# A hybrid attention and SSD layer on one core: an eighth Strassen pair, two filler blocks fewer, a store and a pause moved

## The chip, the cores and the metric

The kernel runs on one core of a Trainium2 chip. The metric is the device time of one execution in microseconds. A measurement of this kernel can tell a difference of some 0.2% from none, which is 3.9 us.

## What is computed

One layer of a streaming encoder, for 1024 prompt tokens and 8 x 16 sample tokens, in 32-bit numbers (1152 tokens stand side by side, `NT`):

```python
h = rms_norm(x, norm_g) * (1 + scale) + shift
q, k, v, z_att, z_ssd, xbc, dt_raw, gates = split(h @ w_in)
att_branch = (attend(rms_norm(q), rms_norm(k), v) * silu(z_att)) @ w_att_proj
xs, bm, cm = split(silu(causal_dwconv(xbc)))
y, h_new = ssd_scan(xs, softplus(dt_raw + dt_bias), a, bm, cm, h0)
y = group_rms_norm((y + d_skip * xs) * silu(z_ssd))
merged = sigmoid(g_att) * att_branch + sigmoid(g_ssd) * (y @ w_ssd_proj)
out = x + gate * (merged @ w_out)
```

The inner width is 2048 for the SSD branch: 32 heads of 64, which the kernel takes in 16 pairs `p` of heads, four pairs to each of four groups that share B and C. The final states of the prompt (`out_hp`) and of the samples (`out_hs`) are outputs too.

## The kernel before

Weights come in blocks of 128 output columns. A **dense block** (`dense`, L474 on) multiplies such a block with all tokens: 8 pieces of the inner dimension, 3 groups of 384 tokens, and 3 products each, since every operand is split into a high and a low part in the fast 32-bit format (L489, L490, L492). That is 72 matmuls of 384 columns a block. The weights' high part is made by ScalarE (L374), the low part by VectorE (L375).

The program has these stages:

- The start: modulation, norm, the first block, four more dense blocks.
- **Strassen pairs** (`pairs`): two dense blocks are made together by Strassen's seven products instead of eight, each of 4 x 2 x 3 matmuls of 288 columns: 168 matmuls a pair (L880, L882, L883). `w_form` makes the sums of the weights on VectorE, the sums of the products are taken by VectorE (L844), activations by ScalarE (L855). `NPR` is the number of pairs, 7. After them one block is left that is made as a plain dense block (L999 and L1000 evict it if it is a z block, L1005 if it is a gate). Results are stored to DRAM and read back where they are needed.
- Attention, 8 units.
- The **SSD stage**, 16 pairs of heads. For each pair PE makes a dense block of x, VectorE runs its causal convolution (three L1531, then L1537 and L1538), and `main` of `ssd(p)` does the scan: transposes (L1754) scaled by VectorE (L1758), products to states (L1799), a chain of 14 small VectorE steps (L1808) that carries the state from chunk to chunk, products to outputs (L1830, L1837, L1855), VectorE steps on them (L1848, L1861, L1862), and the samples' new states (L1881), whose four products each need an operand that GpSimd masks (`masked`, L1788). Only two masked operands are held at a time: the third is made when the first has been used. Each group begins with two dense blocks for B and C with convolutions of their own, and products of them (L1669, L1675). It ends with a norm over the group, whose sums go through DRAM and whose inverse root GpSimd computes (L1156, then lines L328 to L334).
- Six dense blocks of gates, then the projections of attention (`att_dense`), of the SSD branch and of the output. `att_prep` loads the attention results (L1940) and splits them (L1927 on ScalarE, L1929 on VectorE).

**What sets the order.** Everything is written out in one order by a planner in the kernel (`run`). It draws dense matmuls from one generator, keeps a clock that counts the PE time it has written, and slips in steps of the SSD pairs, which wait on that clock (`pause`, `until`) as an allowance for the time that VectorE, ScalarE and GpSimd need. A `pause(4500)` between the second and the third of the samples' four products is such an allowance. The tool that builds the program may move instructions too, by its own schedule. Since a pair of heads needs more time on VectorE than on PE, the planner puts some further dense blocks into the SSD stage as **fillers**: `SLOTS` names the pairs after whose block of x a filler follows. `BLOCKS` is one list of the gate and z blocks: the first `4 + NEARLY` of them are made at the start, the next ones are the fillers, and the gates that are left follow the SSD stage.

Stores from GpSimd (`store`) and loads and stores from SyncE (`dma`) are issued in order, each on its queue, so an instruction that waits there holds up those behind it.

Of the kernel before, what the change touches and what calls it, by code (L numbers as in the profile page):

```python
# [12 lines left out]
P = 128  # L13
# [15 lines left out]
RW = HALO + NP + NB * (HALO + NS)  # L29
EPS = 1e-6  # L30
AHEAD = 2
NEARLY = 15
SLOTS = (('p', 1), ('p', 3), ('p', 6), ('p', 9), ('p', 11), ('p', 13), ('p', 15))
BLOCKS = [("gate", i) for i in range(4)] + [("z", p) for p in range(NPAIR)] + [("gate", i) for i in range(4, 16)]
AHEAD_BLOCKS = BLOCKS[:4 + NEARLY]
FILL = dict(zip(SLOTS, BLOCKS[4 + NEARLY:]))
NGATE = 4 + NEARLY + len(SLOTS) - NPAIR
NZ = 5
NPR = 7
TH = NT // 2  # L40
MH = TH // 2
BIG = -1e30
# [89 lines left out]
def trunk_kernel(ctx: ExitStack, tc: tile.TileContext, h):  # L132
# [182 lines left out]
    store = nc.gpsimd.dma_start  # L315
# [142 lines left out]
    for i in range(NZ):  # L458
        job(h["wall"][i])
    for i in range(NPR):  # L460
        job(*(h["wall"][NZ + 2 * i + j] for j in range(2)))
    for i in range(NZ + 2 * NPR, nz):
        job(h["wall"][i])
# [620 lines left out]
    def pause(t):  # L1084
        yield from until(clock[0] + t)

    def stored(*bufs):

        def wait():
            yield from pause(9000)  # L1090
            for b in bufs:
                b.free()
        urgent.append(wait())
# [520 lines left out]

    ngate = [max(4, 4 + NEARLY - NPAIR)]

# [68 lines left out]
    def ssd(p):  # L1685
# [51 lines left out]
        def main():  # L1737
# [6 lines left out]
            hst = yield from walloc(lay, "T", NP)  # L1744
# [69 lines left out]
            eb = alloc(lay, "T", NT)  # L1814
            for e in range(2):
                dma(eb.ap[e * HD:(e + 1) * HD], eacs_d[hds[e]:hds[e] + 1].to_broadcast([HD, NT]))
            store(h["out_hp"][p], hst.ap[:, 7 * P:])
            yield from pause(1200)
            yield from until(tm)

# [24 lines left out]
            for j in range(3):  # L1845
# [16 lines left out]
                nc.vector.tensor_tensor(x.ap[:, c2], x.ap[:, c2], eb.ap[:, c2], ALU.add)  # L1862
                yield 213 * n
            eb.free()
            stored(hst)
            yield from until(tz)

# [10 lines left out]
            for q in range(4):  # L1878
                j, i = q // 2, q % 2
                for w, b_ in enumerate(res["st"][j]):  # L1880
                    nc.tensor.matmul(pss_[j][:, 2 * i * P:2 * (i + 1) * P], b_.r, xm[q].r, start=w == 0, stop=w == 1)  # L1881
                xm[q].free()
                if q < 2:
                    xm.append(masked(q + 2))
                yield 215
                if q == 1:
                    yield from pause(4500)
                if i:
                    c = slice(4 * j * P, (4 * j + 4) * P)
                    nc.vector.tensor_tensor(h0.ap[:, c], h0.ap[:, c], pss_[j], ALU.add)  # L1890
# [323 lines left out]
```

## Time and profile before

| | |
|---|---|
| median of 3 runs | 1944.68 us (1944.65 to 1945.52) |
| profiled execution | 1943.42 us |
| its span | 1941.6 us |
| PE busy in the span | 1922.7 us (99%) |
| VectorE (DVE) busy | 1251.5 us (64%) |
| ScalarE (ACT) busy | 798.3 us (41%) |
| GpSimd (POOL) busy | 339.7 us (17%) |
| chain that ended last | PE 92%, DVE 3%, DMA 2%, ACT 1% |

The span is what the profile covers of the profiled execution, whose time is 1.8 us longer. PE stands for TensorE's matmuls. Busy shares are means over stages that differ, so a stage is read from the view of its own stretch. Ends of matmuls are modelled; the spacing of their starts is what a matmul costs.

### The profile page before, as it was taken

The numbers are of one execution on the slowest core, as the hardware profiler recorded it, in microseconds if no ns is written. First come the engines' busy times: TensorE is split into PE (matmuls) and PEld (weight loads), VectorE is DVE, ScalarE is ACT, GpSimd is POOL, SyncE is SP. The second block draws the span as 40 slices with busy tenths as digits, with TensorE's granted clock in tenths as the row PEclk, the third lists the DMA queues.
The fourth block names the chain that finished last, engine by engine and source line by source line (L and its number), as shares of the span: only waits on it lengthen the run. The fifth ranks groups of instructions, "written<-read, shape, count | busy, mean of one in ns | idle before, by whom it ended". The sixth has DMA issues, their size and how long they took to land.

```text
span 1941.6 us, 35765 instructions
## 1 busy us (share of the span) xinstructions
PE 1922.7 (99%) x14259; PEld 1842.4 (95%) x14259; DVE 1251.5 (64%) x2577; ACT 798.3 (41%) x1639; POOL 339.7 (17%) x615
## 2 busy tenths in 40 slices
PE   7999999999999999999999999999999999999999
PEld 5999999999899998998999999999999999999999
DVE  6756634555556456558597988888885434777732
ACT  7533324444454444545655546465453311111200
POOL 0000003213123131221022343242241300000000
PEclk9999999999999999999999999999999999999999
DMA  8222342343333333423345354554558742331341
GB/s 316 92 81 95 109 173 69 96 129 116 97 117 101 122 116 94 130 82 115 119 132 181 132 162 152 168 173 140 160 192 289 292 144 93 105 105 56 89 143 52
DMA packets 85966, 258.73 MB, mean 133 GB/s; under 512 B 14732, under 2 KB 15768, under 8 KB 85800
## 3 DMA queue, kind: packets, MB, share of 16 engines
q1 hardware_dynamic: 77416, 229.57, 36.5%
q0 software_dynamic: 8384, 26.88, 3.6%
q8 instruction: 112, 1.84, 0.4%
q14 instruction: 54, 0.44, 0.1%
HBM read 202.72 MB, written 53.68 MB: 132 GB/s over the span
## 4 chain that ended last, share of the span: by engine, by line
PE 92%; DVE 3%; DMA 2%; ACT 1%; issue 1%; POOL 0%; SPq 0%; ACTq 0%; DVEq 0%; POOLq 0%
PE d L489 11%; PE d L492 11%; PE d L490 11%; PE d L557 5%; PE d L555 5%; PE d L556 5%; PE s L489 4%; PE s L490 4%; PE s L492 4%; PE g L1311 3%; PE g L1334 3%; PE s L1390 2%; PE g L880 2%; PE g L883 2%; PE g L882 2%; PE g L490 1%
## 5 line engine op out<-in xcount | busy, mean ns | idle before, releaser
L489 PE MATMUL d<-rarena 128*128 128x384 f32 x1288 | 437.7, 340 | 0.0
L492 PE MATMUL d<-rarena 128*128 128x384 f32 x1288 | 434.2, 337 | 0.0
L490 PE MATMUL d<-rarena 128*128 128x384 f32 x1288 | 433.3, 336 | 0.0
L489 PEld LDWEIGHTS d<-rarena 128*128 128x128 f32 x1288 | 242.0, 188 | 4.1 <-issue 2.7
L492 PEld LDWEIGHTS d<-rarena 128*128 128x128 f32 x1288 | 241.9, 188 | 2.2 <-issue 2.0
L490 PEld LDWEIGHTS d<-rarena 128*128 128x128 f32 x1288 | 242.1, 188 | 0.8 <-issue 0.4
L557 PE MATMUL d<-va_att,rarena 128*128 128x384 f32 (+1 forms) x567 | 197.6, 349 | 0.0
L555 PE MATMUL d<-va_att,rarena 128*128 128x384 f32 (+1 forms) x567 | 196.7, 347 | 0.0
L556 PE MATMUL d<-va_att,rarena 128*128 128x384 f32 (+1 forms) x567 | 193.7, 342 | 0.0
L374 ACT ACTIVATE rarena<-arena 128x1024 fp32r<-128x1024 f32 x76 | 80.5, 1059 | 262.9 <-PE s L490 173.9
L489 PE MATMUL s<-rarena 128*128 128x384 f32 x488 | 165.6, 339 | 0.0
L490 PE MATMUL s<-rarena 128*128 128x384 f32 x488 | 164.2, 336 | 0.0
L492 PE MATMUL s<-rarena 128*128 128x384 f32 x488 | 163.3, 335 | 0.0
L1299 ACT ACTIVATE ma_att<-ma_att 128x640 f32<-128x640 f32 (+2 forms) x144 | 101.5, 706 | 135.8 <-DVE ma_att L1408 99.7
L1228 POOL TENSOR_SCALAR ma_att<-ma_att 128x16 f32<-128x16 f32 (+1 forms) x24 | 5.2, 218 | 707.3 <-DVE ma_att L1205 417.2
L557 PEld LDWEIGHTS d<-va_att,rarena 128*128 128x128 f32 x567 | 107.0, 189 | 3.9 <-issue 2.7
L555 PEld LDWEIGHTS d<-va_att,rarena 128*128 128x128 f32 x567 | 106.8, 188 | 2.7 <-issue 1.2
L375 DVE TENSOR_TENSOR rarena<-arena,rarena 128x1024 fp32r<-128x1024 f32 x76 | 93.3, 1227 | 22.6 <-ACT rarena L374 22.6
L556 PEld LDWEIGHTS d<-va_att,rarena 128*128 128x128 f32 x567 | 106.8, 188 | 0.5
L1531 DVE SCALAR_TENSOR_TENSOR ma_att<-ma_att,arena 128x1176 f32<-128x1176 f32 x63 | 93.9, 1491 | 9.4 <-ACT ma_att L1528 8.1
L489 PEld LDWEIGHTS s<-rarena 128*128 128x128 f32 x488 | 91.7, 188 | 1.3 <-issue 1.2
L490 PEld LDWEIGHTS s<-rarena 128*128 128x128 f32 x488 | 91.7, 188 | 0.8 <-issue 0.8
(437 smaller groups left out, 4128.0 us busy)
## 6 DMA issues: line engine op xcount, KB each, us to landing
arena<-in_wall_dram SPq DMA_DIRECT2D x85, 512.0 KB, 3.6
ma_att<-in_kc_dram SPq DMA_DIRECT2D x64, 256.0 KB, 4.3
ma_att<-in_vc_dram SPq DMA_DIRECT2D x64, 256.0 KB, 3.5
ma_att<-acs_d SPq DMA_DIRECT2D x23, 576.0 KB, 6.8
ma_att<-y_d SPq DMA_DIRECT2D x15, 576.0 KB, 6.3
arena<-in_wssd_dram SPq DMA_DIRECT2D x16, 512.0 KB, 4.5
z_d<-va_start SPq DMA_DIRECT2D x13, 576.0 KB, 2.8
ma_att<-eacs_d SPq DMA_DIRECT2D x26, 288.0 KB, 3.9
```

The source lines that it names most:

```text
L374: keep(nc.scalar.activation(hi.r[:, c], b.ap, AF.Copy))
L375: keep(nc.vector.tensor_tensor(lo.r[:, c], b.ap, hi.ap[:, c], ALU.subtract))
L489: nc.tensor.matmul(ps, hi.r[:, wc], kh.r[:, tok], start=k == 0, stop=False)
L490: nc.tensor.matmul(ps, hi.r[:, wc], kl.r[:, tok], start=False, stop=False)
L492: nc.tensor.matmul(ps, lo.r[:, wc], kh.r[:, tok], start=False, stop=k == nk - 1)
L555: nc.tensor.matmul(ps, kh.r[:, tok], wh, start=j == 0, stop=False)
L556: nc.tensor.matmul(ps, kh.r[:, tok], wl, start=False, stop=False)
L557: nc.tensor.matmul(ps, kl.r[:, tok], wh, start=False, stop=j == KT - 1)
L1299: nc.scalar.activation(p, p, AF.Exp, bias=sm_[:, 4 + e:5 + e], scale=-1.0, accum_out=sm_[:, 6 + e:7 + e])
L1311: nc.tensor.transpose(ps[:, s * P:(s + 1) * P], p[:, (j + s) * P:(j + s + 1) * P], ident)
L1334: late(nc.tensor.matmul(po[e * HD:e * HD + HD, a * P:(a + 1) * P], v.ap[:, vc:vc + HD], x.ap[:, o + i * P:o + (i + 1) * P], start=i == 0, ...
L1531: nc.vector.scalar_tensor_tensor(yc, r.ap[:, j:j + n], w4[:, i, j:j + 1], yc, ALU.mult, ALU.add)
```

## The change

- `NEARLY` goes from 15 to 17 and `NPR` from 7 to 8: two more blocks are made at the start, and all but one of the blocks after the first five are made in pairs. The blocks made at the start are now gates 0 to 3, all z blocks, and gate 4; the plain block after the pairs is gate 4, where it was z block 14.
- `SLOTS` has five entries where it had seven. The fillers are now gates 5 to 9, where they were z block 15 and gates 4 to 9. `NGATE` stays 10, so six gate blocks still follow the SSD stage.
- The store of the prompt's final state of a pair of heads is written some steps later, behind the VectorE steps on the outputs.
- The pause between the two halves of the samples' products is 6500 in place of 4500 on the planner's clock.

```diff
--- before.py
+++ after.py
@@ -29,14 +29,14 @@
 RW = HALO + NP + NB * (HALO + NS)
 EPS = 1e-6
 AHEAD = 2
-NEARLY = 15
-SLOTS = (('p', 1), ('p', 3), ('p', 6), ('p', 9), ('p', 11), ('p', 13), ('p', 15))
+NEARLY = 17
+SLOTS = (('p', 1), ('p', 3), ('p', 6), ('p', 10), ('p', 15))
 BLOCKS = [("gate", i) for i in range(4)] + [("z", p) for p in range(NPAIR)] + [("gate", i) for i in range(4, 16)]
 AHEAD_BLOCKS = BLOCKS[:4 + NEARLY]
 FILL = dict(zip(SLOTS, BLOCKS[4 + NEARLY:]))
 NGATE = 4 + NEARLY + len(SLOTS) - NPAIR
 NZ = 5
-NPR = 7
+NPR = 8
 TH = NT // 2
 MH = TH // 2
 BIG = -1e30
@@ -1814,7 +1814,6 @@
             eb = alloc(lay, "T", NT)
             for e in range(2):
                 dma(eb.ap[e * HD:(e + 1) * HD], eacs_d[hds[e]:hds[e] + 1].to_broadcast([HD, NT]))
-            store(h["out_hp"][p], hst.ap[:, 7 * P:])
             yield from pause(1200)
             yield from until(tm)
 
@@ -1862,6 +1861,7 @@
                 nc.vector.tensor_tensor(x.ap[:, c2], x.ap[:, c2], eb.ap[:, c2], ALU.add)
                 yield 213 * n
             eb.free()
+            store(h["out_hp"][p], hst.ap[:, 7 * P:])
             stored(hst)
             yield from until(tz)
 
@@ -1884,7 +1884,7 @@
                     xm.append(masked(q + 2))
                 yield 215
                 if q == 1:
-                    yield from pause(4500)
+                    yield from pause(6500)
                 if i:
                     c = slice(4 * j * P, (4 * j + 4) * P)
                     nc.vector.tensor_tensor(h0.ap[:, c], h0.ap[:, c], pss_[j], ALU.add)
```

Since the planner writes the order, the change moves instructions in the whole SSD stage. Up to the end of the seventh pair the order of PE is the same. Two places follow.

GpSimd's queue at the end of the third group, where the group's norm (L1156, L328 to L334) and the masks of pair 12 (L1788, the four operands of its products) meet; L1817 is the store of the prompt's state, L1639 that of a gate. Before:

```order
L1156 TENSOR_SCALAR ma_att<-ma_att 128x9
L328 MEMSET ma_att 128x9
L329 TENSOR_TENSOR ma_att<-ma_att 128x9
L331 TENSOR_TENSOR ma_att<-ma_att 128x9
L332 TENSOR_TENSOR ma_att<-ma_att 128x9
L333 TENSOR_SCALAR ma_att<-ma_att 128x9
L334 TENSOR_TENSOR ma_att<-ma_att 128x9
L1817 DMA out_hp_dram<-va_ssd 128x128
L331 TENSOR_TENSOR ma_att<-ma_att 128x9
L1788 TENSOR_TENSOR rarena<-rarena,arena 128x256
L332 TENSOR_TENSOR ma_att<-ma_att 128x9
L1788 TENSOR_TENSOR rarena<-rarena,arena 128x256
```

And now:

```order
L1156 TENSOR_SCALAR ma_att<-ma_att 128x9
L328 MEMSET ma_att 128x9
L329 TENSOR_TENSOR ma_att<-ma_att 128x9
L331 TENSOR_TENSOR ma_att<-ma_att 128x9
L1788 TENSOR_TENSOR rarena<-rarena,arena 128x256 x2
L332 TENSOR_TENSOR ma_att<-ma_att 128x9
L333 TENSOR_SCALAR ma_att<-ma_att 128x9
L1639 DMA gate_d<-ma_att 128x384
L334 TENSOR_TENSOR ma_att<-ma_att 128x9
L331 TENSOR_TENSOR ma_att<-ma_att 128x9
L332 TENSOR_TENSOR ma_att<-ma_att 128x9
L333 TENSOR_SCALAR ma_att<-ma_att 128x9
```

The two L1788 in each piece are the third and fourth mask of pair 12. They stood behind eight and nine instructions of the norm (L1156 counted) and the store of the state; now they stand behind four, and the store is ahead of the norm.

SyncE's queue near the end of the SSD stage: L1940 loads attention results for `att_dense`, L1960 results of the SSD pairs, L1948 gates, L2005 modulation weights, L350 weights, and L1842 (now L1841) the z block of pair 15. Before:

```order
L1940 DMA ma_att<-att_d 128x1152
L1816 DMA ma_att<-eacs_d 64x1152 x2
L350 DMA arena<-in_wall_dram 128x1024
L1960 DMA va_ssd<-y_d 128x1152
L1940 DMA va_ssd<-att_d 128x1152 x2
L350 DMA arena<-in_watt_dram 128x1024
L1940 DMA ma_att<-att_d 128x1152
L1955 DMA va_ssd<-yb_11520 128x1152
L1940 DMA ma_att<-att_d 128x1152
L1842 DMA va_ssd<-z_d 128x1152
L1940 DMA ma_att<-att_d 128x1152
L1948 DMA ma_att<-gate_d 128x1152 x3
```

And now:

```order
L1816 DMA va_ssd<-eacs_d 64x1152 x2
L2005 DMA va_ssd<-in_wada_dram 128x1024
L1960 DMA ma_att<-y_d 128x1152
L1841 DMA va_ssd<-z_d 128x1152
L1948 DMA ma_att<-gate_d 128x1152
L1960 DMA ma_att<-y_d 128x1152
L1948 DMA ma_att<-gate_d 128x1152 x2
L1960 DMA ma_att<-y_d 128x1152
L1940 DMA va_ssd<-att_d 128x1152
L350 DMA arena<-in_watt_dram 128x1024
L2005 DMA va_ssd<-in_wada_dram 128x1024
L1940 DMA va_ssd<-att_d 128x1152
```

The last two loads of attention results stood ahead of the gates and right beside the z block of pair 15; now they stand behind it, behind gates and behind results of the SSD pairs.

## Rows read from the trace of the kernel before

**Rows 1.** the page, parts 1 and 2: engines; busy tenths of 40 slices
```profile
PE 1922.7 (99%) x14259; PEld 1842.4 (95%) x14259; DVE 1251.5 (64%) x2577; ACT 798.3 (41%) x1639; POOL 339.7 (17%) x615
...
DVE  6756634555556456558597988888885434777732
```

**Rows 2.** waits of PE: line, releaser, us in all, times, longest
```profile
PE g L634 <- DMA m<-in_xT_dram: 8.5, 2, 8.3
PE g L1881 <- POOL rarena L1788: 2.1, 2, 1.2
PE g L1675 <- DVE ma_att L1537: 1.4, 1, 1.4
...
PE g L1830 <- DVE ma_att L1808: 0.7, 1, 0.7
...
PE g L1855 <- DVE ma_att L1848: 0.2, 1, 0.2
```

**Rows 3.** stretches: PE, PEld, DVE, ACT, POOL busy us (x), clock, DMA, GB/s
```profile
1000.40:1433.90 433.50, 429.03 (x3342) 419.08 (x3339) 379.68 (x631) 230.60 (x481) 144.66 (x235) 1.00 0.49 159
1093.40:1131.30 37.90, 37.90 (x294) 36.51 (x288) 36.45 (x61) 21.72 (x46) 11.25 (x19) 1.00 0.43 137
1325.80:1433.90 108.10, 106.05 (x815) 102.96 (x813) 94.37 (x152) 57.89 (x119) 35.77 (x60) 1.00 0.47 152
...
1650.00:1700.00 50.00, 50.00 (x290) 50.00 (x289) 39.31 (x61) 8.90 (x9) 0.00 (x0) 1.00 0.32 102
```

**Rows 4.** line L880 of the pairs: ns min/median/max, first and last start
```profile
L880 PE MATMUL g<-rarena x168: 288/295/297, 102.3 to 258.5; 128*128 128x288 f32 x168
```

**Rows 5.** lines L375 and L1626, VectorE's share of a moved block
```profile
L375 DVE TENSOR_TENSOR rarena<-arena,rarena x76: 1209/1224/1527, 73.9 to 1914.0; 128x1024 fp32r<-128x1024 f32 x76
...
L1626 DVE SCALAR_TENSOR_TENSOR ma_att<-ma_att,d x2: 544/547/550, 970.2 to 978.3; 128x384 f32<-128x384 f32 x2
...
L1531 DVE SCALAR_TENSOR_TENSOR ma_att<-ma_att,arena 128x1176 f32<-128x1176 f32 x33 | 49.5, 1500 | 7.9 <-ACT ma_att L1528 7.5
```

**Rows 6.** VectorE's waits from 1000 to 1434 us, the longest ones
```profile
DVE ma_att L1531 <- ACT ma_att L1528: 8.1, 5, 2.5
DVE ma_att L1733 <- ACT ma_att L1731: 6.7, 5, 4.5
DVE ma_att L1758 <- PE g L1754: 6.5, 3, 3.1
```

**Rows 7.** timeline of POOL and PE, 1408 to 1417 us: start, us, engine, line
```profile
1408.13 0.20 POOL L1156 TENSOR_SCALAR ma_att<-ma_att 128x9 f32<-128x9 f32 x1 [8.35 <-DMA ma_att<-ya]
...
1408.57 1.90 POOL L329 TENSOR_TENSOR ma_att<-ma_att 128x9 f32<-128x9 f32 x1
...
1413.08 0.63 POOL L1817 DMA_DIRECT2D out_hp_dram<-va_ssd  x1
...
1413.89 0.68 POOL L1788 TENSOR_TENSOR rarena<-rarena,arena 128x256 fp32r<-128x256 f32 x1
...
1414.70 1.77 POOL L1788 TENSOR_TENSOR rarena<-rarena,arena 128x256 fp32r<-128x256 f32 x1
...
1414.63 0.51 PE L1881 MATMUL g<-rarena 128*128 128x256 f32 x2 [1.18 <-POOL rarena L1788]
```

**Rows 8.** line L1788 of POOL: ns min/median/max, first and last start
```profile
L1788 POOL TENSOR_TENSOR rarena<-rarena,arena x64: 605/656/1832, 989.1 to 1512.4; 128x256 fp32r<-128x256 f32 x64
```

**Rows 9.** timeline of VectorE, 1075 to 1082 us
```profile
1075.75 3.16 DVE L1531 SCALAR_TENSOR_TENSOR ma_att<-ma_att,arena 128x1176 f32<-128x1176 f32 x2
...
1080.25 1.22 DVE L1537 SCALAR_TENSOR_TENSOR ma_att<-ma_att 128x1024 f32<-128x1024 f32 x1 [0.74 <-ACT ma_att L1533]
1081.39 0.28 DVE L1538 SCALAR_TENSOR_TENSOR ma_att<-ma_att 128x128 f32<-128x128 f32 x1
```

**Rows 10.** issues of L1940 by SP, and first and last of L1929 on VectorE
```profile
L1940 SPq DMA_DIRECT2D ma_att<-att_d x6: 319/320/787, 1441.9 to 1497.7; - x6
...
L1929 DVE TENSOR_TENSOR rarena<-va_ssd,rarena x7: 1349/1353/1359, 1526.1 to 1844.3; 128x1152 fp32r<-128x1152 f32 x7
```

## The prediction

> **What bounds the kernel now.** I read the engines' busy shares first: PE is busy for 99% of the span, VectorE for 64% [rows 1]. So PE is the bound, and a change can save only PE time or one of PE's few waits. The slices show that the 64% is a mean over unlike stages: VectorE is at 8 or 9 tenths from the 20th slice to the 29th, which is the SSD stage, and at 5 to 7 before it [rows 1]. Next come PE's waits [rows 2]. Most of their sum lies at the start (8.5 us on the load of x), which the change does not touch. In the SSD stage PE waits 4.4 us: 2.1 on GpSimd's masks (L1788), 1.4 on VectorE in the head of a group (L1537), 0.9 in two more places. Last I read stretches [rows 3]. From the first state products (L1837) of pair 0 to those of pair 13, at 1000.4 and 1433.9 us, VectorE is busy 379.7 of 433.5 us, which is 87.6%. The reader should see that PE hides VectorE there with little to spare: 54 us of VectorE's idle time in 433. All fillers that the change takes out stood in or beside this stage. The granted clock is 1.00 in all these stretches, so the clock has no term.
>
> **The change part by part.** The sum is made against the profiled execution, 1943.42 us, which is 1.26 us under the median of the runs.
>
> *The eighth pair.* The seven pairs have 7 x 168 = 1176 matmuls, back to back; from the first to the 1174th pass 156.2 us [rows 4], so 133.2 ns each and 22.4 us a pair. Plain dense work shows 290 matmuls in 50 us [rows 3], 172.4 ns each, so a block of 72 takes 12.4 us and two take 24.8. One pair in place of two blocks saves 2.4 to 2.5 us; I take **-2.5**. The Trainium skill ("TensorE: Matmul & The Clock Gate", section "Back-to-back issue gap") gives a spacing of N/2.4 + 2.5 ns for one matmul behind another, which is 122.5 ns for 288 columns and 162.5 for 384; by that the estimate would be -2.8. The trace has some 10 ns more in each, and by it I go. The pair's additions, splits and activations on VectorE and ScalarE lie under PE as those of the other seven do; if that cover failed, its share would be a few waits of under 1 us, the length of one such step.
>
> *What leaves the SSD stage.* Two blocks, 144 matmuls or 24.8 us of PE, and with them two weight splits on VectorE of 1.22 us each [rows 5]. A z filler becomes a gate, which has no L1626: three times 0.55 us less [rows 5]. So VectorE loses 4 us there and its cover loses 25. By the two orders the planner spreads this out. From the first L1837 of pair 0 to that of pair 13, PE had 1744 dense matmuls and has 1703: 41 x 0.1724 = 7.1 us less cover, for about the same VectorE work. The rest lies ahead of pair 0 (34 matmuls fewer) and behind pair 15 (78 fewer), where the gate blocks and the attention projection are the cover. Inside, the loss is uneven. Up to pair 10 there are 42 matmuls more; from pair 10 to pair 13 there are 350 where there were 433. In that stretch before, VectorE was busy 94.4 of 108.1 us and PE 106.05 [rows 3]. Now PE has 106.05 - 83 x 0.1724 = 91.7 us of work, and VectorE has one L375, three L1531 and one L1538 fewer (1.22 + 3 x 1.5 + 0.28 = 6.0 us [rows 5, 9]), so 88.4. That is 96%. Can VectorE run so full? For 38 us from 1093.4 it did, 36.45 of 37.9 with PE at no wait [rows 3], but not for 92. Its waits are on ScalarE more than on PE, the longest single sum of 8.1 us being on L1528 [rows 6]. A wait on PE vanishes when VectorE is late, one on ScalarE only in part. **Bounds:** nothing, if VectorE closes up as it did at 1093; and if it keeps its 13.7 us of idle time, 88.4 + 13.7 - 91.7 = 10.4 us. I keep three fifths of the idle time (the share that I give to ScalarE), which is 8.2 us and leaves PE 4.9 us behind; of that I take 2 off, as the 42 extra matmuls up to pair 10 let VectorE start this stretch less late. **+3.0.**
>
> *The masks.* In the timeline of pair 12 GpSimd starts the group's norm at 1408.13, and the store of the state and the third mask of the samples come only at 1413.08 and 1413.89; PE wants that mask and waits 1.18 us, and again for the fourth [rows 7], 2.1 us in all [rows 2]. GpSimd's order now has four instructions of the norm ahead of these masks, not eight and nine, and the store is no longer among them. The first three of these, through L329, took to 1410.5. So the masks should be there some 2 to 3 us sooner, at much the same PE cover (23 dense matmuls between the halves, 22 before). Elsewhere the longer pause gives 42 matmuls where there were 30 for most pairs, 2 us more cover, which buys nothing since those pairs did not wait. Bounds -2.1 and 0; I take **-1.8**. The later store itself costs nothing on GpSimd: its issue is the same 0.6 us [rows 7], and behind it stand halos, stores and masks that have until the next pair.
>
> *The head of the second group.* At 1081.5 PE waits 1.4 us for the convolution of C: VectorE goes through two L1531 and then L1537 and L1538, with one gap of 0.74 us [rows 9]. Ahead of it, between pair 0 and pair 2, the order now has 229 dense matmuls where it had 195, 5.9 us more PE time, for some 3 us more VectorE work. So VectorE comes less late. Bounds -1.4 and 0; I take **-1.0**. The other 0.9 us stay.
>
> *The end of the stage.* The last two loads of attention results now stand behind the load of pair 15's z. The last load was issued at 1497.7 and its split ran from 1526.1 on [rows 10]: 28 us to spare, of which the 78 matmuls take 13.4. I cost it at nothing; if it did come late, the eighth operand would be late in a block that takes them one by one.
>
> Sum: -2.5 + 3.0 - 1.8 - 1.0 = **-2.3 us**, so 1942.4 against the median of 1944.68.
>
> **The rivals.**
> 1. *No new wait.* VectorE closes up fully and all 4.4 us of waits go: -2.5 - 4.4 = -6.9 us, 1937.8. For it: the 96% at 1093 without a wait. Against it: 92 us is more than twice that length.
> 2. *VectorE becomes the bound between pairs 10 and 13.* It keeps its idle time and PE waits 10.4 us there, at the transposes' products (L1799) and in the fourth group's head. With the mask and head terms gone as above that is -2.5 - 2.8 + 10.4 = +5.1 us, 1949.8: slower. It decides from where new waits exceed 9.2 us (3.9 + 2.5 + 2.8), that is if VectorE cannot get above 88.4/100.9 = 87.6%. For it: this is its share over the whole 433 us. Against it: that share was never demanded to be more, since PE hid it.
> 3. *The masks turn tight elsewhere.* In five pairs (0, 6, 10, 11, 12) the order has only 22 to 25 dense matmuls between the halves, 3.8 us at the least. A mask takes 0.66 us in the median but up to 1.83 [rows 8]; a store of 0.63 [rows 7] and two slow masks make 4.3, so 0.5 us in each, 2.5 in all: the sum becomes +0.2, 1944.9. For it: the fuller VectorE. Against it: the median. The Trainium skill ("GPSIMD Engine Reference", section "Key points") says that GpSimd shares its SBUF interfaces with VectorE and contends with instructions of two SBUF inputs, which most of VectorE's are; no run here yet shows that this makes the slow masks.
>
> **How the numbers follow.** A measurement of this kernel tells 0.2%, 3.9 us, from no change. My forecast has 0.45 (from -4.5 to +1), rival 1 has 0.32, rival 2 has 0.15, rival 3 has 0.08. Faster by over 3.9 us is rival 1 and a tail of the forecast: 0.36. Slower is rival 2: 0.15. The rest, 0.49, is within. The range goes down to rival 1 in full, 1937.8, and up to where rival 2 has been entered, 1948.6.
>
> **What would show it.** Right: eight times 168 matmuls at 133 ns; no wait of PE on L1788 over 1 us; the wait on L1537 at the second group's head gone or under 0.5 us; new waits of PE on VectorE of some 3 us in all, most between pairs 10 and 13, where VectorE is above 90%. Wrong: no waits at all there (rival 1), one long chain of waits there (rival 2), waits on L1788 in several pairs (rival 3), or a wait of the attention projection on its operands.

## The result, and the profile after

The changed kernel takes 1946.32 us in the median of 22 runs, the kernel before in the same comparison 1943.95 us: a ratio of 1.0019, with a 95% interval from 1.0012 to 1.0027. In a second comparison on another chip (the first run of the second group below) it was 1.0028, from 1.0017 to 1.0039. So it is slower, by some 4 to 5 us by the ratios (2.4 and 4.4 by the medians), where the prediction had 2.3 us faster.

The profiled execution took 1945.71 us, its span is 1943.9 us. The page, parts 1 and 2, for the changed kernel:

```profile
PE 1921.7 (99%) x14283; PEld 1839.0 (95%) x14283; DVE 1257.6 (65%) x2593; ACT 800.5 (41%) x1645; POOL 323.9 (17%) x609
...
DVE  7756652555555565557678888989986534777732
```

The shares are those of before [rows 1]: the page doesn't show the loss. The pairs are as forecast. Line L880 of the changed kernel (ns min/median/max, first and last start):

```profile
L880 PE MATMUL g<-rarena x192: 288/295/297, 100.9 to 279.5; 128*128 128x288 f32 x192
```

From the first to the 1342nd of their 1344 matmuls pass 178.6 us, 133.2 ns each as before [rows 4].

The waits of PE in the SSD stage of the changed kernel (960 to 1640 us; line, releaser, us in all, times, longest):

```profile
PE g L1881 <- POOL rarena L1788: 3.7, 1, 3.7
PE g L1675 <- DVE ma_att L1537: 0.7, 1, 0.7
PE g L1829 <- DVE ma_att L1808: 0.6, 1, 0.6
PE g L1669 <- DVE ma_att L1677: 0.6, 1, 0.6
PE g L1799 <- DVE qa_ssd L1890: 0.5, 1, 0.5
PE g L1799 <- DVE ma_att L1758: 0.5, 1, 0.5
PE g L1829 <- ACT ma_att L1533: 0.5, 1, 0.5
PE g L1799 <- ACT va_ssd L1670: 0.4, 1, 0.4
PE g L1829 <- PE g L1829: 0.2, 1, 0.2
```

They sum to 7.7 us where they were 4.4 [rows 2]. The wait on the masks, which was to go, grew from 2.1 to 3.7, in one piece. Five short ones on VectorE and ScalarE are new.

The stretches that answer to [rows 3]: pair 0 to pair 13, pairs 6 to 9, pairs 10 to 13, and 3.4 us right behind the wait on the masks (busy us of PE, PEld, DVE, ACT, POOL with counts, clock, DMA share, GB/s):

```profile
1015.10:1447.00 431.90, 424.27 (x3291) 411.52 (x3287) 377.63 (x631) 229.07 (x477) 134.06 (x232) 1.00 0.50 158
1212.70:1317.10 104.40, 101.17 (x784) 96.42 (x781) 92.81 (x156) 54.57 (x117) 28.39 (x55) 1.00 0.51 158
1350.40:1447.00 96.60, 92.91 (x731) 89.92 (x728) 87.05 (x154) 52.49 (x113) 33.21 (x56) 0.98 0.49 158
...
1431.95:1435.35 3.40, 3.25 (x11) 3.25 (x12) 1.35 (x2) 3.35 (x7) 2.75 (x9) 0.50 0.14 58
```

And of the kernel before, pairs 6 to 9, and a piece of its start:

```profile
1192.80:1294.60 101.80, 101.01 (x794) 98.58 (x792) 91.13 (x153) 54.16 (x115) 33.06 (x57) 1.00 0.50 158
...
30.10:33.40 3.30, 3.30 (x18) 2.90 (x21) 2.51 (x4) 2.37 (x7) 0.00 (x0) 0.50 1.03 412
```

The reader should see four things. From pair 0 to pair 13, PE has 41 dense matmuls (7.1 us) less, by the two orders, and the stretch is only 1.6 us shorter: PE's idle time in it went from 4.5 us (433.5 - 429.03) to 7.6 (431.9 - 424.27). Between pairs 6 and 9 the idle time went from 0.8 to 3.2 us. Between pairs 10 and 13 it is 3.7 us, all of it the one wait on the masks. And behind that wait the granted clock is 0.50 for 3.4 us, the lower of its two levels (1.2 GHz), which costs half of that in PE's work, 1.7 us. The kernel before has such a stretch too in its profiled execution, but at its start, at 30 us, where the changed one has none. So the spans differ by 2.3 us only, and some 4 when this is put aside.

The half clock is not of this one execution. The mean granted clock was below 1.000 (0.997 to 0.999) in all 28 runs of the changed kernel, the six of the second comparison among them. There it was 0.9983 in the mean, against 0.9998 in the 20 runs of the kernel before on the same chip; the difference, 0.0014 of 1944 us, is 2.8 us of PE's work.

The changed kernel where the third group's norm meets the masks of pair 12, a timeline of PE, SP and POOL (start, us, engine, line; in brackets the idle time before):

```profile
1414.11 0.85 PE L1142 MATMUL g<-va_ssd,arena 128*32 128x384 f32 x6
...
1416.95 0.83 SPq L1147 DMA_DIRECT2D ya<-va_ssd  x3
...
1421.31 0.43 SPq L1155 DMA_DIRECT2D ma_att<-ya  x1
...
1423.78 0.63 PE L1881 MATMUL g<-rarena 128*128 128x256 f32 x4
1425.60 1.46 POOL L1156 TENSOR_SCALAR ma_att<-ma_att 128x9 f32<-128x9 f32 x1 [6.69 <-DMA ma_att<-ya]
...
1427.29 1.83 POOL L329 TENSOR_TENSOR ma_att<-ma_att 128x9 f32<-128x9 f32 x1
1429.20 1.08 POOL L331 TENSOR_TENSOR ma_att<-ma_att 128x9 f32<-128x9 f32 x1
1430.24 2.37 POOL L1788 TENSOR_TENSOR rarena<-rarena,arena 128x256 fp32r<-128x256 f32 x2
...
1432.10 0.80 PE L1881 MATMUL g<-rarena 128*128 128x256 f32 x2 [3.69 <-POOL rarena L1788]
```

PE makes the norm's sums (L1142) at 1414.1. They are stored and loaded again, and GpSimd stands for 6.69 us at the norm's first instruction (L1156) until that load has landed; the masks are queued behind it and start as soon as the four instructions ahead of them are done. The second mask is done at 1432.6, 18.5 us after the sums; PE goes on with the first at 1432.1, 18.0 us after them. It wanted that one at 1428.4, 14.3 us after the sums, since only 44 dense matmuls stand between the sums and the second half of the products. The sums in the kernel before:

```profile
1396.82 0.85 PE L1142 MATMUL g<-va_ssd,arena 128*32 128x384 f32 x6
```

There PE went on with the first late mask at 1414.63, 17.8 us after the sums, and had wanted it 1.18 us earlier [rows 7], 16.6 us after them, with 54 dense matmuls between. So the chain through GpSimd is as long as before, and PE's work over it is 2.3 us shorter.

### The profile page after: what moved, and what is told of

It is laid out like the page before. It is cut to its first block, busy times and chain, and to the rows that moved or that the text cites. A ratio compares the mean times of both kernels' runs of the same rounds, so it can differ in the third digit from the quotient of the medians.

```text
span 1943.9 us, 35821 instructions
## 1 busy us (share of the span) xinstructions
PE 1921.7 (99%) x14283; PEld 1839.0 (95%) x14283; DVE 1257.6 (65%) x2593; ACT 800.5 (41%) x1645; POOL 323.9 (17%) x609
## 4 chain that ended last, share of the span: by engine, by line
PE 91%; DVE 4%; DMA 2%; ACT 2%; issue 1%; POOL 0%; SPq 0%; ACTq 0%; DVEq 0%
PE d L489 10%; PE d L492 10%; PE d L490 10%; PE d L557 5%; PE d L555 5%; PE d L556 5%; PE s L489 4%; PE s L492 4%; PE s L490 4%; PE g L1311 3%; PE g L1334 3%; PE g L880 2%; PE g L883 2%; PE g L882 2%; PE s L1390 2%; PE g L1829 1%
## 5 line engine op out<-in xcount | busy, mean ns | idle before, releaser
L489 PE MATMUL d<-rarena 128*128 128x384 f32 x1256 | 428.1, 341 | 0.0
L492 PE MATMUL d<-rarena 128*128 128x384 f32 x1256 | 423.4, 337 | 0.0
L490 PE MATMUL d<-rarena 128*128 128x384 f32 x1256 | 423.3, 337 | 0.0
L489 PEld LDWEIGHTS d<-rarena 128*128 128x128 f32 x1256 | 236.4, 188 | 3.5 <-issue 3.0
L490 PEld LDWEIGHTS d<-rarena 128*128 128x128 f32 x1256 | 236.5, 188 | 1.6 <-issue 1.2
L492 PEld LDWEIGHTS d<-rarena 128*128 128x128 f32 x1256 | 236.2, 188 | 1.0 <-issue 0.8
L489 PE MATMUL s<-rarena 128*128 128x384 f32 x472 | 160.2, 339 | 0.0
L492 PE MATMUL s<-rarena 128*128 128x384 f32 x472 | 159.0, 337 | 0.0
L490 PE MATMUL s<-rarena 128*128 128x384 f32 x472 | 158.4, 336 | 0.0
L375 DVE TENSOR_TENSOR rarena<-arena,rarena 128x1024 fp32r<-128x1024 f32 x74 | 90.9, 1228 | 30.0 <-ACT rarena L374 29.9
L1531 DVE SCALAR_TENSOR_TENSOR ma_att<-ma_att,arena 128x1176 f32<-128x1176 f32 x63 | 93.5, 1484 | 4.4 <-ACT ma_att L1528 3.3
L489 PEld LDWEIGHTS s<-rarena 128*128 128x128 f32 x472 | 88.7, 188 | 1.5 <-issue 1.4
L492 PEld LDWEIGHTS s<-rarena 128*128 128x128 f32 x472 | 88.7, 188 | 0.2 <-issue 0.2
```

Source lines behind the costliest of these rows:

```text
L375: keep(nc.vector.tensor_tensor(lo.r[:, c], b.ap, hi.ap[:, c], ALU.subtract))
L489: nc.tensor.matmul(ps, hi.r[:, wc], kh.r[:, tok], start=k == 0, stop=False)
L490: nc.tensor.matmul(ps, hi.r[:, wc], kl.r[:, tok], start=False, stop=False)
L492: nc.tensor.matmul(ps, lo.r[:, wc], kh.r[:, tok], start=False, stop=k == nk - 1)
L1531: nc.vector.scalar_tensor_tensor(yc, r.ap[:, j:j + n], w4[:, i, j:j + 1], yc, ALU.mult, ALU.add)
```

## The experiments

All ratios are to the kernel before on the same chip, with 95% intervals. The theories are named in the expectations, which were written before each run. Theory 1 of the first group was that the pair is worth its 2.5 us and that what is lost was lost for want of the fillers' cover.

| run | pairs | fillers | pause, store | masks | ratio | interval |
|---|---|---|---|---|---|---|
| changed | 8 | 5 | 6500, late | POOL | 1.0019 | 1.0012 to 1.0027 |
| e1 | 8 | 7 | 4500, early | POOL | 0.9990 | 0.9978 to 1.0001 |
| e2 | 8 | 5 | 6500, late | POOL, norm later | 1.0010 | 0.9999 to 1.0020 |
| e3 | 7 | 7 | 6500, late | POOL | 0.9996 | 0.9986 to 1.0005 |
| e4 | 8 | 5 | 4500, early | POOL | 1.0001 | 0.9990 to 1.0011 |
| e5 | 8 | 5 | 6500, late | POOL | 1.0028 | 1.0017 to 1.0039 |
| e6 | 8 | 5 | 4500, late | POOL | 1.0024 | 1.0014 to 1.0034 |
| e7 | 8 | 5 | 6500, early | POOL | 1.0037 | 1.0025 to 1.0049 |
| e8 | 8 | 7 | 4500, early | some on ACT | 0.9981 | 0.9973 to 0.9990 |
| e9 | 8 | 5 | 6500, late | some on ACT | 1.0006 | 0.9997 to 1.0015 |
| e10 | 8 | 7 | 6500, late | POOL | 0.9983 | 0.9974 to 0.9991 |
| e11 | 8 | 5 | 4500, early | some on ACT | 0.9999 | 0.9989 to 1.0009 |
| e12 | 8 | 8 | 4500, early | some on ACT | 1.0056 | 1.0044 to 1.0069 |
| e13 | 8 | 5, last at 12 | 6500, late | POOL | 1.0018 | 1.0009 to 1.0027 |
| e14 | 8 | 5, at 9 and 12 | 6500, late | POOL | 1.0001 | 0.9990 to 1.0011 |
| e15 | 8 | 7 | 6500, late | some on ACT | 0.9989 | 0.9981 to 0.9998 |

### First group: the parts of the change

**e1, the eighth pair with all seven fillers** (against the changed kernel; pause and store are those of before):

```diff
-SLOTS = (('p', 1), ('p', 3), ('p', 6), ('p', 10), ('p', 15))
+SLOTS = (('p', 1), ('p', 3), ('p', 6), ('p', 9), ('p', 11), ('p', 13), ('p', 15))
-                    yield from pause(6500)
+                    yield from pause(4500)
```

> Eight pairs, but the seven fillers of before (two gates come from the six that follow the SSD stage, so four follow), with the pause and the store as before. Theory 1 (the pair saves 2.5 us, the loss comes from PE's waits in the SSD stage once fillers are gone): the SSD stage keeps the waits of before (4.4 us), so 2 to 3 us faster than before. Theory 2 (an eighth pair costs elsewhere what it saves): no faster than before, within 1 us. If the SSD stage now ends too late for the attention projection, new waits of PE show after pair 15, and it is slower than before.

Measured: 0.9990, about 2 us faster, with an interval that just reaches 1. The pair's term holds as far as this can tell. PE waits 4.1 us on masks here, in four pieces, at the masks of pairs 8 and 12.

**e2, the norm begun later:**

```diff
 def rsqrt_dram(d0, d1, nrow, width, b):
-        yield from pause(2300)
+        yield from pause(9000)
```

> The changed kernel, with the first pause of the group's norm 9000 in place of 2300, so that GpSimd masks the samples' operands of pair 12 before it waits for the norm's sums. Dense order on PE unchanged. Theory 1: the 3.7 us wait of PE on the mask goes, the others stay: 3 to 4 us faster than the changed kernel, within 1 us of before. Theory 3 (VectorE bounds the stage with five fillers, and the mask wait only happens to be where PE is held): the wait comes back within a few us as waits on VectorE, less than 1 us is gained.

Measured: 1.0010, between the two theories. No wait on masks is left in the trace, but there are 1.9 us on a ScalarE step (L1638, a gate's activation) at 1464 us, with a half-clock stretch behind it, and 1.8 us on L1890 (0.5 in the changed kernel) at 1172 and 1310 us. In ten of the twelve runs the mean clock is 1.000, so most have no such stretch. So the wait was real, and a part of it came back; the interval overlaps that of the changed kernel's first comparison, not that of its second.

**e3, the pause and the store without the pair and with all fillers:**

```diff
-NEARLY = 17
-SLOTS = (('p', 1), ('p', 3), ('p', 6), ('p', 10), ('p', 15))
-NPR = 8
+NEARLY = 15
+SLOTS = (('p', 1), ('p', 3), ('p', 6), ('p', 9), ('p', 11), ('p', 13), ('p', 15))
+NPR = 7
```

> The kernel before (seven pairs, seven fillers) with only the two small edits: the longer pause and the later store. Theory 1: there are 72 dense matmuls, not 54, between the third group's sums and the second half of the samples' products, so the 2.1 us wait on the masks goes: 1.5 to 2.5 us faster than before. Theory 3: the same or slightly slower, as neither edit moves work off VectorE.

Measured: 0.9996, no difference, and so a miss. The wait on masks is gone from the trace; between pairs 6 and 8 PE now waits 1.7 us at L1799, on L1758, L1890 and L1670, where it did not before.

**e4, the changed kernel without pause and store:**

```diff
-                    yield from pause(6500)
+                    yield from pause(4500)
```

and the store back at its old place.

> The changed kernel without its two small edits: eight pairs, five fillers, pause and store as before. The second half of the samples' products comes 46 dense matmuls after the third group's sums (44 in the changed kernel, 54 before), but the masks now stand behind seven instructions of the norm. Theory 1: a wait on the masks of 4 to 6 us, so 0 to 2 us slower than the changed kernel. If the small edits are what costs, it is faster than the changed kernel by more than 1 us.

Measured: 1.0001, faster than the changed kernel, where theory 1 had it 0 to 2 us slower; PE waits 2.9 us on the masks of pair 12, not 4 to 6. With five fillers the two edits cost some 3 to 5 us, while with seven (e3) they cost nothing that this can tell. The half clock does not make that difference: all twelve runs of e4 have a mean clock of 0.998 or 0.999 too.

### Second group: which edit costs, and another engine for the masks

**e5, the changed kernel once more.** 

> The changed kernel once more, unchanged, on the chip of the next three, so that they can be set against it. All theories: a ratio of 1.0015 to 1.0025 to the kernel before (1.0019 first), PE waiting about 3.7 us on the masks (L1788) of pair 12 and 0.4 to 0.6 us in five or six places on VectorE and ScalarE between pairs 6 and 9, and one stretch of 3.41 us at half the granted clock behind the wait on the masks. If the ratio comes out at 1.000, the loss was of that one chip or of chance.

Measured: 1.0028, a little above the range expected. The loss is there on another chip. Behind the same wait of 3.7 us the clock is at half for 6.8 us here.

**e6, pause 4500, store late; e7, pause 6500, store early.** Each undoes one of the two edits alone.

> The changed kernel with the pause of 4500 again; the store stays late. Theory P (the longer pause costs: the sums of the samples' states, L1890, move into the next pair's first steps on VectorE, and the PSUM buffers of the products with them): the small waits between pairs 6 and 9 on L1677, L1670 and L1890 go, PE's excess there falls from about 7 to about 5 us, and the kernel is 2 to 3.5 us faster than the changed one, as the run with both small edits undone was. Theory S (the later store costs): it stays as slow as the changed kernel. Theory N (neither; only spread): both this and the next run are within 1 us of the changed kernel.

> The changed kernel with the store of the prompt's state at its old place; the pause stays at 6500. The order of PE is word for word that of the changed kernel. Theory P: within 1 us of the changed kernel, with the same waits between pairs 6 and 9. Theory S: 2 to 3.5 us faster than it.

Measured: 1.0024 and 1.0037. Neither theory P nor theory S holds by itself: with five fillers either edit alone is as bad as both. The traces show two places. In e7 the wait on the masks of pair 12 (3.7 us) is that of the changed kernel, and the waits between pairs 6 and 9 are much the same, but for one on L1890 that is longer (1.4 us where it was 0.5). In e6 GpSimd's queue stands somewhere else, in pair 13 (timeline of POOL, and the waits of PE from 1440 to 1480 us):

```profile
1465.82 0.54 POOL L1639 DMA_DIRECT2D gate_d<-ma_att  x1 [5.48 <-ACT ma_att L1638]
1466.38 2.33 POOL L1788 TENSOR_TENSOR rarena<-rarena,arena 128x256 fp32r<-128x256 f32 x2
...
PE g L1881 <- POOL rarena L1788: 3.5, 2, 2.4
```

Here the masks stand behind the store of a gate (L1639), which waits for ScalarE. The same order does no harm in e4, where that store is 4 us earlier and PE waits for nothing from 1440 to 1480. It came back in e11 (3.0 us at the same place). Why the store's place shifts ScalarE so far there was not settled.

**e8, seven fillers, and ScalarE makes the third and fourth mask of each group's first pair** (against e1):

```diff
                 i = 2 * (q % 2)
+                if q >= 2 and p % PPG == 0:
+                    for b in range(2):
+                        nc.scalar.activation(t.r[:, b * P:(b + 1) * P], xs[q // 2].ap, AF.Copy, scale=bmask4[:, i + b:i + b + 1])
+                    return t
```

> Eight pairs, seven fillers, pause 4500 and early store (as the run that gave 0.9990), and the third and fourth mask of the first pair of each group made by ScalarE (two activations of 128 columns each, some 0.39 us by L1727's form) where GpSimd made them behind the norm. Theory 1 (the masks wait on GpSimd's queue, behind a norm that waits for its data): PE's 4.1 us of waits on L1788 fall to the one or two of pairs that are not first in a group, under 1.5 us, and the kernel gains 2 to 4 us on that run: 1937 to 1939 where the kernel before is at 1942.4, ratio 0.997 to 0.9985, more where a stretch at half clock goes with them. Rival (the wait moves to ScalarE's queue, or to VectorE, as in the run with the norm delayed): waits of 1.5 to 3 us on ScalarE or on L1890 take their place, ratio 0.9985 to 0.9995.

Measured: 0.9981, by the medians 3.6 us faster than the kernel before; the gain on e1, 0.0009, lies within the intervals of the two. One such activation takes 0.39 us, and PE's waits on the masks fall from 4.1 to 0.3 us (L1790 of ScalarE; then two of the waits of PE, in which lines from 1790 on are four higher):

```profile
L1790 ACT ACTIVATE rarena<-rarena,arena x16: 383/388/392, 1026.4 to 1437.9; 128x128 fp32r<-128x128 f32 x16
...
PE g L1859 <- DVE ma_att L1852: 1.1, 1, 1.1
...
PE g L1885 <- ACT rarena L1790: 0.3, 1, 0.3
```

### Third group: fillers against masks

**e9, the changed kernel with ScalarE's masks; e11, e4 with them** (the diff of e8 in each).

> The changed kernel with the third and fourth mask of each group's first pair made by ScalarE; nothing else is altered. Theory M (what the changed kernel lost is mostly the wait on the masks behind the norm, 3.7 us, and the 3.41 us at half clock that follow it, 1.7 us of work): both go, and the ratio to the kernel before falls from 1.0019 or 1.0028 to between 0.9993 and 1.0003. Theory C (with 25 us less PE work in the stage the waits come back on VectorE and ScalarE, as they did when the norm was delayed): no wait on masks, but 3 us or more of waits on VectorE and ScalarE after pair 12, a half-clock stretch in another place, and a ratio of 1.0007 to 1.0018.

> Eight pairs and five fillers, pause 4500 and early store, with ScalarE's masks: the run that gave 1.0001 less its waits on masks. Theory M: PE's waits of 2.9 us on masks and the half-clock stretch behind them go, 0.9980 to 0.9993. Theory C: waits on L1890 and L1848 grow in their place, 0.9995 to 1.0005. Against the run with seven fillers and ScalarE's masks (0.9981) it also prices the two fillers with the masks out of the way: nothing by Theory M, 2 us or more by Theory C.

Measured: 1.0006, between the ranges of the two theories, and 0.9999. With the changed kernel's pause and store ScalarE's masks give back part of the loss (1.0019 and 1.0028 to 1.0006); at e4 they give nothing (1.0001 to 0.9999). Waits on L1638 (two, 2.3 us) and L1890 (1.2 us; four lines further down in that kernel) appear in e9, and the masks of pair 13, which GpSimd still makes, hold PE in e11. Theory C has more of the truth: one wait mended, others come. Two fillers more at the same masks (e8 against e11) are worth 0.0018, 3.5 us.

**e10, the changed kernel with seven fillers** (the first two lines of e1's diff and nothing else).

> The changed kernel with seven fillers in place of five (all at the places of before; four gates follow the stage), so eight pairs, pause 6500 and late store. Theory A (the pause and the store cost only where the fillers are gone): as the run with seven fillers and neither edit, ratio 0.9985 to 0.9998, waits of the stage under 5 us. Theory B (the two edits cost some 3 us with eight pairs whatever the fillers): 1.0008 to 1.0020, with waits of PE on L1890 and L1677 between pairs 6 and 9 of 2 us and more.

Measured: 0.9983. This is theory A, and it is the plainest of the runs: three entries more and one less in one list, which move two gate blocks from behind the stage into it, turn the change from slower to faster, by 0.0036 to 0.0045 (7 to 9 us). Its timeline at the third group's norm:

```profile
1422.72 0.85 PE L1142 MATMUL g<-va_ssd,arena 128*32 128x384 f32 x6
...
1435.17 1.25 POOL L1156 TENSOR_SCALAR ma_att<-ma_att 128x9 f32<-128x9 f32 x1 [5.22 <-DMA ma_att<-ya]
...
1438.73 2.17 POOL L1788 TENSOR_TENSOR rarena<-rarena,arena 128x256 fp32r<-128x256 f32 x2
...
1441.49 0.64 PE L1881 MATMUL g<-rarena 128*128 128x256 f32 x4
```

GpSimd is no faster and its masks stand behind the same four instructions of the norm: 18.2 us from the sums to the end of the second mask (18.5 in the changed kernel). But PE has 72 dense matmuls in between and wants them 18.8 us after the sums. It does not wait for them; 5.0 us of other waits are left in the stage.

**e12, an eighth filler on e8:**

```diff
-SLOTS = (('p', 1), ('p', 3), ('p', 6), ('p', 9), ('p', 11), ('p', 13), ('p', 15))
+SLOTS = (('p', 1), ('p', 3), ('p', 6), ('p', 8), ('p', 9), ('p', 11), ('p', 13), ('p', 15))
```

> The fastest run so far (eight pairs, seven fillers, ScalarE's masks, 0.9981) with an eighth filler: fillers after pairs 1, 3, 6, 8, 9, 11, 13 and 15, so three gates follow the stage. If the 2.7 us that PE still waits there are cover that VectorE lacks, up to 2 us more: 0.9970 to 0.9978. If those waits have other causes (order, a step on ScalarE), the same as before within 1 us, 0.9976 to 0.9986.

Measured: 1.0056, 11 us slower and outside both expectations. The waits of PE and a stretch of its clock:

```profile
PE d L489 <- DVE va_ssd L1981: 4.2, 1, 4.2
PE g L489 <- ACT rarena L1931: 4.2, 1, 4.2
...
1531.80:1541.90 10.10, 5.91 (x21) 5.61 (x20) 4.35 (x6) 2.33 (x2) 0.00 (x0) 0.50 0.84 307
```

L1931 (L1927 in the other kernels) splits the attention results, L1981 evicts the attention projection. At the first wait PE comes to that projection before an operand is split; at the second VectorE is late with an eviction, behind two weight splits (L375) and one more step. Three gates stand behind the stage here in place of four; that this is the reason is likely, but no run separates it.

### Fourth group: number or place

**e13, the last filler at pair 12 in place of 15; e14, the fourth also at 9 in place of 10:**

```diff
-SLOTS = (('p', 1), ('p', 3), ('p', 6), ('p', 10), ('p', 15))
+SLOTS = (('p', 1), ('p', 3), ('p', 6), ('p', 10), ('p', 12))
```

> The changed kernel with its five fillers, the last moved from pair 15 to pair 12; pause, store and the other four as changed. The order of PE is the same up to the end of pair 11; between the sums of the third group's norm and the second half of pair 12's products it has 92 dense matmuls where the changed kernel has 44, and GpSimd's order has both late masks of pair 12 ahead of the norm. Theory L (place: the loss is the missing cover between pairs 10 and 13, where the norm's round trip meets the masks): the wait of 3.7 us on L1788 and the half-clock stretch behind it go, 5.4 us or somewhat more, and the ratio falls to 0.9985 to 1.0000; the small waits between pairs 6 and 9 stay, since the order there is the same. Theory F (number: five fillers are too few wherever they stand): waits on VectorE come up elsewhere, and it stays at 1.0010 to 1.0030.

> As the run before it, with the fourth filler moved from pair 10 to pair 9 as well (where the kernel before has one): fillers after pairs 1, 3, 6, 9 and 12. Theory L: 0.9980 to 0.9998, with the waits between pairs 8 and 9 smaller (half of the 2 us that pair 8 loses). Theory F: 1.0010 to 1.0030.

Measured: 1.0018, in theory F's range, and 1.0001, between the two. In e13 the wait on the masks falls to 1.2 us and no half-clock stretch follows it, as theory L had it. But in the profiled execution, the slowest of its 11 runs, a wait and a stretch stand at the end of the stage (waits of PE, and the clock there), and the waits on L1890 have grown from 0.5 to 2.5 us:

```profile
PE g L489 <- ACT rarena L1927: 2.1, 1, 2.1
PE g L1881 <- POOL rarena L1788: 1.2, 1, 1.2
...
1554.70:1558.10 3.40, 3.40 (x11) 3.40 (x12) 1.26 (x1) 0.00 (x0) 0.00 (x0) 0.50 0.64 227
```

The wait is for a split of attention results, whose last load is issued at 1540.7 us; in e14, which has no block behind pair 15 either, it is issued at 1530.1 and that wait is not there. So the missing block alone does not make it. Between e13 and e14 the place of one filler is worth some 3 us, but no place that was tried makes five as good as seven.

**e15, e10 with ScalarE's masks.** 

> The run with eight pairs, seven fillers, the longer pause and the later store (0.9983), with ScalarE's masks for the first pair of each group on top. That run had no wait on masks left, so if masks are all that ScalarE's masks mend, nothing changes: 0.9978 to 0.9988. If the freer GpSimd queue helps VectorE too (the shorter span of the run with ScalarE's masks and the old pause, 1935.8 us), 0.9968 to 0.9978.

Measured: 0.9989, no gain over e10 (the intervals overlap). Where PE's cover already hides the masks, another engine for them buys nothing that this can tell.

The fastest are e8 (0.9981) and e10 (0.9983), which these runs can't tell apart. Both beat the kernel before and the changed one. e10 is the changed kernel with its `SLOTS` as they were.

## Why the prediction was wrong

**The pair was right.** 133.2 ns a matmul, 2.5 us by the traces; e1 against the kernel before gives 2 us, and the ratios of e10 and e3 differ by 0.0013 (2.5 us).

**The masks' step failed:** "Bounds -2.1 and 0; I take -1.8." Measured: a wait longer by 1.6 us, and with the half-clock stretch behind it 3.3 us. Two readings carried the step. By GpSimd's order the masks were to come "some 2 to 3 us sooner", since fewer instructions of the norm stand ahead of them. They came no sooner: from the start of L1156 to PE's next product pass 6.5 us (1425.60 to 1432.10), as before (1408.13 to 1414.63 [rows 7]). Four instructions and the store went, but L1156 takes 1.46 us where it took 0.20, and the first mask 1.80 where it took 0.68. And "much the same PE cover" was taken from the matmuls between the two halves. But GpSimd stands at L1156 until a round trip through DRAM is over, and that trip starts with PE's own sums. What had to be counted was PE's work from the sums to the products that need the masks: 44 matmuls where there were 54, 14.3 us where there were 16.6, against a chain of 18.0 where it was 17.8 (18.0 in e4 too, with seven instructions of the norm ahead of the masks). A sign of it stood in [rows 7]: 8.35 us at L1156, until the load of `ya`. Of this, rival 3 had the place (pair 12 was in its list), at 0.5 us. The two orders that stand ahead of the prediction could not show it; a count in PE's order could.

**The term for lost cover had some of its size and the wrong place:** "+3.0", "between pairs 10 and 13". VectorE was busy 87.05 us there, near the 88.4 forecast, and PE waited for it nowhere in the stretch: the only wait is the one on GpSimd. Rival 2 has the right sign and fails on the same point. The new idle time lies between pairs 6 and 9, 2.4 us, with PE as busy as before (101.17 and 101.01 us) and VectorE 1.7 us more.

**The pause was not free:** "2 us more cover, which buys nothing since those pairs did not wait". It also moves the sums on the samples' states (L1890) later among VectorE's steps. Between pairs 6 and 8 the kernels with 6500 and seven fillers (e3, e10) wait 1.7 us and 2.2 us in L1799 and L1754; e1 and e8, with 4500, wait there not at all and for 1.1 us. With seven fillers this shows in no ratio (e3; e10 against e1). With five, the pause alone costs 0.0036, 7 us (e7 against e4).

**The later store was not free either:** it "costs nothing on GpSimd". With five fillers and the old pause it costs 0.0023, 4.5 us (e6 against e4).

**The clock was put at nothing:** "The granted clock is 1.00 in all these stretches, so the clock has no term." That was read from stretches without a long wait. Measured: 1.7 us in the profiled execution, 2.8 us by the mean clocks of the second comparison.

**The head of the second group** came out at -0.7 us where -1.0 was taken. **The end of the stage** was rightly costed at nothing: no wait of the projection in the changed kernel. Its margin was small, as the waits there in e12 and e13 show.

**The sum.** From pair 0 to pair 13: 7.1 us of matmuls out by the orders, 3.2 us of PE's idle time and 1.7 us of half clock in, and 0.6 us that these don't account for, which makes the 1.6 us by which that stretch is shorter. The 7.1 us of matmuls are not saved, since those blocks stand elsewhere. Against the pair's 2.5 us stand 4.9 us of idle time and clock there; that gives 2.4 of the measured 4 to 5 us. With the 2.8 us by which the mean clock of the runs differs, in place of the 1.7 of this execution, it is 3.5; the rest is not in one place that the views show. By the runs, two fillers at the same edits are worth 7 to 9 us (e10 against the changed kernel and e5), 2 us where pause and store are as before (e1 against e4). My estimate of the whole lost cover was 3.0. That the measured 1946.32 us lies inside my range is luck: the range reached up to the rivals' times, and the sum had the sign wrong.

**Two misreadings that changed nothing:** VectorE's run of slices at 8 or 9 tenths goes from the 21st to the 30th, with a 7 in the 22nd, and those before the 21st go from 3 to 8 [rows 1]. And instructions with two SBUF inputs, "which most of VectorE's are" by rival 3, make some 60% of VectorE's busy time between pair 0 and pair 13 of the kernel before, but only some 40% of its instructions.

What stays open: why pause and store, each alone, cost as much as both with five fillers. The traces of e6 and e7 show two places that tip, the masks of pair 13 and those of pair 12; that one edit moves the first and the other the second was seen in one profiled execution each.

## What to carry to other kernels

Where an engine's in-order queue holds an instruction that waits for a round trip, count the bound engine's work from the start of that trip to the first use of what is queued behind it; the number of queued instructions says little. Dense blocks put among tight stages as cover are worth more than their place in PE's sum: before one is taken out, look for each chain that it hides, and price a wait with the half-clock stretch that may follow it. And test a schedule's small edits together with the cover that they will have, since the same two edits showed no cost here with seven fillers and some 4 us with five.

## What the runs showed of the hardware

A wait of PE can cost more than its length. In the changed kernel the granted clock falls to 0.50 (1.2 GHz) within the wait of 3.7 us and stays there for 3.4 us, though the view of waits has none for PE in the 110 us before (1318 to 1428). In the profiled executions of e2, e4, e5, e6, e7, e11, e12, e13 and e14 the longest wait of PE in or right behind the stage is between 1.8 and 4.2 us, and each has such a stretch in it or up to 2.5 us behind it, of 3.4 us or more. In those of the kernel before, e3, e8, e9, e10 and e15 the longest is 1.4 us, and none has one there; e1 has one behind two waits of 1.2 us each, and none behind its single longest, 1.5 us. In e12 the first stretch begins at 1531.7 us, behind three waits of 0.7 to 0.9 us since 1526.5 and ahead of the wait of 4.2. Nor do waits of some 2 us bring a stretch each time: by the mean clocks two of the twelve runs of e2 can have one, and all twelve of e4. So a wait of the longer kind is to be priced with half of that stretch on top, as in all 28 runs of the changed kernel; for one of some 2 us that is the upper bound.

GpSimd's masks take from 0.60 to 1.84 us in the changed kernel, and VectorE has a part in it. In e1 two of them took 4.18 us, while VectorE ran instructions with two SBUF inputs (timeline of POOL and DVE):

```profile
1259.24 4.18 POOL L1788 TENSOR_TENSOR rarena<-rarena,arena 128x256 fp32r<-128x256 f32 x2
...
1259.89 1.35 DVE L1733 TENSOR_TENSOR va_ssd<-va_ssd,ma_att 128x1152 f32<-128x1152 f32 x1
1261.16 1.79 DVE L1531 SCALAR_TENSOR_TENSOR ma_att<-ma_att,arena 128x1176 f32<-128x1176 f32 x1
```

Two places in the changed kernel, the first late mask of pair 12 and, at 1236 us, two masks that took 1.19 us together; and line L1531 of VectorE (ns min/median/max):

```profile
1430.13 1.44 DVE L1531 SCALAR_TENSOR_TENSOR ma_att<-ma_att,arena 128x1176 f32<-128x1176 f32 x1
...
1430.24 1.80 POOL L1788 TENSOR_TENSOR rarena<-rarena,arena 128x256 fp32r<-128x256 f32 x1
...
1236.24 2.63 DVE L1531 SCALAR_TENSOR_TENSOR ma_att<-ma_att,arena 128x1176 f32<-128x1176 f32 x1
...
1236.43 1.19 POOL L1788 TENSOR_TENSOR rarena<-rarena,arena 128x256 fp32r<-128x256 f32 x2
...
L1531 DVE SCALAR_TENSOR_TENSOR ma_att<-ma_att,arena x63: 1426/1439/2630, 983.1 to 1430.1; 128x1176 f32<-128x1176 f32 x63
```

Of the 64 masks of the changed kernel, 20 took over 1 us, and each of these ended 0.47 us behind the end of such an instruction of VectorE. The mask at 1430.24 is one of them (1431.57 and 1432.04). At 1236 us it went the other way: both masks were fast and lay wholly within one L1531, and that one took 2.63 us where the median is 1.44, longer by the 1.19 us of the two masks. So one engine stands still for the other; which of the two, their starts do not tell, since L1531 began first in both places. The Trainium skill ("GPSIMD Engine Reference", section "Key points") has GpSimd share its SBUF interfaces with VectorE, with contention where VectorE's instruction has two SBUF inputs. The trace agrees, at the 20 slow masks and at the long L1531. The mask that PE waited for in the changed kernel is one of the slow ones; rival 3 had named "the fuller VectorE" for this.
